# Row sums of a 64 MiB tensor: another split of the rows into a contiguous lead and a pitched body

## The chip, the cores and the metric

The kernel runs on one core of one Trainium2 chip. The metric is the device time of one execution in microseconds (us). Before the change three runs gave 160.83, 160.84 and 161.1 us, median 160.84.

The engines that matter here are VectorE (DVE in the profile), ScalarE (ACT), and SyncE (SP), which computes nothing and issues the transfers; sixteen DMA engines move the data between HBM and the on-chip memory of 128 partitions.

## What is computed

The reference sums the last axis of a float32 tensor and scales the sums:

```
batch, seq, dim = 32, 512, 1024
x = randn(batch, seq, dim).astype(float32);  multiplier = 0.5
out = (np.sum(x, axis=-1) * multiplier).astype(np.float32)
```

That is 16384 rows of 1024 numbers, 4 KiB a row, 67.1 MB to read and 64 KiB of results to write.

## The kernel before, in words

With 128 partitions each partition takes 128 rows. The rows are cut into two regions of the input. The first region has 112 rows per partition (`own`, line 42): partition p owns rows 112p to 112p+111, so that neighbouring partitions read at a pitch of 112 rows (448 KiB). The second region, `x_last`, is the contiguous end of the input, 16 rows per partition at a pitch of 16 rows (64 KiB).

The first region is read in seven blocks of B = 16 rows per partition (64 KiB a partition, 8 MiB a block). Three buffers `xb0` to `xb2` take turns. The loop of line 108 issues each block's load on SP (`load`, line 73, the DMA at line 76); from block 3 on a load first waits until VectorE has reduced the block that had the buffer before (`freed`). The first three loads wait for nothing, and `start_loads_at_entry` moves them into the entry of the program. All loads and stores are issued by SP and go through one queue in order of issue.

For each block VectorE waits for the load, reduces it in one instruction (line 121, 16 sums per partition into `sums`), and scales the sums into `res` (line 127). The seventh block is halved: VectorE reduces its first 8 rows, ScalarE the other 8, one row an instruction, as a scaled copy with an accumulator (`act_row`, line 85).

The last region is the tail, and is loaded in pieces, so that the work behind the last byte is small: 10 rows; 4 rows; one row and the first 384 columns of the last row (lines 146 to 158); then columns 384 to 735 of the last row, and columns 736 to 1023, both into the small tile `end` (lines 159 to 167). The waits at their issue keep buffer reuse in order: the tail's buffer must have been freed (line 143), the third piece's load waits for block 5's reduce, the last piece's for block 6's. In the tail VectorE and ScalarE share the rows. VectorE sums a row in one instruction that adds its two halves and accumulates (`dve_sum`, line 95); ScalarE has the rows in `on_act` (line 174). The last row is summed by VectorE in three cuts, the last of which also takes in the two partial sums, which lie in `end` just ahead of that cut's data (lines 185 to 192).

The results leave in two stores, both issued by SP. The early one (line 169) writes the 112 columns of the first region when block 6 has been summed. The last one (line 195) writes the 16 columns of the tail when the last sum is there. SP then waits for both to land (lines 199 and 200).

Of the kernel before, what the change touches and what calls it, by code (L numbers as in the profile page):

```python
# [8 lines left out]
@with_exitstack  # L9
def kernel(  # L10
    ctx: ExitStack,
    tc: tile.TileContext,
    x: bass.AP,
    multiplier: float,
    out: bass.AP,
):

    nc = tc.nc
    tc.close()
    tc.compile()  # L26
    nc.switch_body("work")

    P = nc.NUM_PARTITIONS
    fp32 = mybir.dt.float32  # L30
    ADD = mybir.AluOpType.add

    x_flat = x.flatten_outer_dims()
    N, D = x_flat.shape
    rows = N // P
    out_flat = out.rearrange("b s -> (b s)")
    mul = float(multiplier)

    B = 16
    n_blocks = rows // B  # L40
    assert N == P * rows and rows == n_blocks * B
    own = rows - B
    x_rows = x_flat[0 : P * own, :].rearrange("(p c) d -> p c d", p=P)
    x_last = x_flat[P * own : N, :].rearrange("(p c) d -> p c d", p=P)
    out_rows = out_flat[0 : P * own].rearrange("(p c) -> p c", p=P)
    out_last = out_flat[P * own : N].rearrange("(p c) -> p c", p=P)

    def sbuf(name, *shape):
        return ctx.enter_context(nc.sbuf_tensor(name, list(shape), fp32)).ap()

    bufs = 3
    buf = [sbuf(f"xb{i}", P, B, D) for i in range(bufs)]
    sums = sbuf("sums", P, rows)
    res = sbuf("res", P, rows)
    cuts = [384, 736, D]
    at = 368
    end = sbuf("end", P, at + D - cuts[1])

    def sem(name):
        return nc.alloc_semaphore(name=name)  # L60

    dve_done = sem("dve_done")
    act_done = sem("act_done")
    counts = {"dve": 0, "act": 0}

    def marks(i, engine):

        s = dve_done if engine == "dve" else act_done
        i.then_inc(s, 1)
        counts[engine] += 1  # L70
        return counts[engine]

    def load(name, dst, src, free=None, behind=None):

        landed = sem(name)
        i = nc.sync.dma_start(out=dst, in_=src)  # L76
        if free is not None:
            i.wait_op(dve_done, free, "sem-ge")
        if behind is not None:
            i.wait_op(behind, 16, "sem-ge")  # L80
        i.then_inc(landed, 16)
        return landed

    def act_row(t, r, col):
        return nc.scalar.activation(  # L85
            out=t[:, r, :],
            in_=t[:, r, :],
            func=mybir.ActivationFunctionType.Copy,
            scale=mul,
            accum_out=res[:, col : col + 1],  # L90
        )

    def dve_sum(row, dst, scale):
        mid = row.shape[-1] // 2
        return nc.vector.tensor_tensor_reduce(  # L95
            out=row[:, 0:mid],
            in0=row[:, 0:mid],
            in1=row[:, mid:],
            scale=scale,
            scalar=0.0,  # L100
            op0=ADD,
            op1=ADD,
            accum_out=dst,
        )

    freed = []
    blocks = []
    for b in range(n_blocks - 1):
        c0 = b * B
        t = buf[b % bufs]  # L110
        landed = load(
            f"landed{b}",
            t,
            x_rows[:, c0 : c0 + B, :],
            freed[b - bufs] if b >= bufs else None,
        )
        blocks.append(landed)
        h = B if b < n_blocks - 2 else B // 2
        nc.vector.wait_ge(landed, 16)
        done = marks(  # L120
            nc.vector.reduce_sum(  # L121
                out=sums[:, c0 : c0 + h], in_=t[:, 0:h, :], axis=mybir.AxisListType.X
            ),
            "dve",
        )
        freed.append(done)
        scaled = nc.vector.tensor_single_scalar(  # L127
            out=res[:, c0 : c0 + h],
            in_=sums[:, c0 : c0 + h],
            scalar=mul,  # L130
            op=mybir.AluOpType.mult,
        )
        scaled.wait_op(dve_done, done, "sem-ge")
        early_dve = marks(scaled, "dve")
        if h < B:
            nc.scalar.wait_ge(landed, 16)
            for r in range(h, B):
                i = act_row(t, r, c0 + r)
            early_act = marks(i, "act")

    c0 = (n_blocks - 1) * B
    t = buf[(n_blocks - 1) % bufs]
    nc.sync.wait_ge(dve_done, freed[n_blocks - 1 - bufs])
    flat = t.rearrange("p c d -> p (c d)")
    flat_last = x_last.rearrange("p c d -> p (c d)")
    bounds = [0, 10 * D, 14 * D, 15 * D + cuts[0]]

    landed = [
        load(f"landed_p{k}", flat[:, lo:hi], flat_last[:, lo:hi], free, behind)
        for k, (lo, hi, free, behind) in enumerate(  # L150
            zip(
                bounds[:-1],
                bounds[1:],
                (None, None, freed[n_blocks - 3]),
                (None, blocks[n_blocks - 3], None),
            )
        )
    ]
    landed_end = [
        load(f"landed_e{k}", end[:, to : to + hi - lo], x_last[:, B - 1, lo:hi], free, behind)  # L160
        for k, (to, lo, hi, free, behind) in enumerate(
            (
                (0, cuts[0], cuts[1], None, blocks[n_blocks - 2]),
                (at, cuts[1], D, freed[n_blocks - 2], None),
            )
        )
    ]
    nc.sync.wait_ge(dve_done, early_dve)
    early = nc.sync.dma_start(out=out_rows, in_=res[:, 0:own])
    early.wait_op(act_done, early_act, "sem-ge")  # L170
    early_stored = sem("early_stored")
    early.then_inc(early_stored, 16)

    on_act = {1, 4, 7, 9, 13, 14}
    for k, (lo, hi) in enumerate(((0, 10), (10, 14), (14, 15))):
        on = [r for r in range(lo, hi) if r in on_act]
        nc.scalar.wait_ge(landed[k], 16)
        for r in on:
            i = act_row(t, r, c0 + r)
        late_act = marks(i, "act") if k == len(landed) - 1 else None  # L180
        on = [r for r in range(lo, hi) if r not in on_act]
        nc.vector.wait_ge(landed[k], 16)
        for r in on:
            dve_sum(t[:, r, :], res[:, c0 + r : c0 + r + 1], mul)
    dve_sum(t[:, B - 1, 0 : cuts[0]], end[:, at - 2 : at - 1], 1.0)
    nc.vector.wait_ge(landed_end[0], 16)
    second = dve_sum(end[:, 0 : cuts[1] - cuts[0]], end[:, at - 1 : at], 1.0)

    second.then_inc(landed_end[1], 1)
    final = dve_sum(end[:, at - 2 :], res[:, rows - 1 : rows], mul)  # L190
    final.wait_op(landed_end[1], 17, "sem-ge")
    done = marks(final, "dve")

    nc.sync.wait_ge(act_done, late_act)
    store = nc.sync.dma_start(out=out_last, in_=res[:, own:])
    store.wait_op(dve_done, done, "sem-ge")
    stored = sem("stored")
    store.then_inc(stored, 16)
    nc.sync.wait_ge(early_stored, 16)
    nc.sync.wait_ge(stored, 16)  # L200

    def start_loads_at_entry(nc_):

        entry, *rest = nc_.main_func.blocks
        is_sp = lambda i: i.engine == mybir.EngineType.SP
        is_load = lambda i: type(i).__name__ == "InstDMACopy"
        for block in rest:
            body = list(block.instructions)  # L210
            own = [i for i in body if is_sp(i)]
            if not any(is_load(i) for i in own):
                continue
            lead = []
            for i in own:
                if not is_load(i) or i.sync_info.on_wait:
                    break
                lead.append(i)
            names = {i.name for i in lead}
            block.instructions = [i for i in body if i.name not in names]  # L220
            head = list(entry.instructions)
            at = next(
                k for k, i in enumerate(head) if is_sp(i) and type(i).__name__ == "InstDrain"
            )
            entry.instructions = head[:at] + lead + head[at:]
            return

    nc.at_finalize(start_loads_at_entry)
# [35 lines left out]
```

## Time and profile before

| | us |
|---|---|
| median of three runs | 160.84 |
| span of the profiled execution, first to last instruction | 159.3 |
| VectorE busy | 119.8 |
| ScalarE busy | 16.3 |
| VectorE waiting for blocks (line 121) | 33.3 in 7 waits |
| one block's reduce | 17.22 |
| scaling of a block's sums | 0.17 |
| a row on ScalarE, with its accumulator read | 1.04 |
| a row on VectorE in the tail, start to start | 0.61 |
| early store, issue to landing | 10.6 |
| last store, issue to landing | 1.4 |

The profile is of one execution; the time of that execution outside its span isn't given separately, and the median of the runs is 1.5 us above the span. In the rows, L121 is line 121 of the kernel, "xb<-in_x_dram" a transfer from the input into a buffer, and the bracket at the end of a timeline line tells how long the engine stood idle before the instruction and what it waited for. The digits are tenths of busy time in 40 slices of the span. Of SP, the profile shows the issues of transfers and what they waited for. TensorE isn't used.

### The profile page before, as it was taken

The page shows a single profiled execution, that of the slowest core. Times are in us where ns is not written, and L with a number is a line of the kernel's source. Part 1 is how long each engine was busy: PE and PEld are TensorE (multiplying, and loading weights), DVE is VectorE, ACT ScalarE, POOL GpSimd, SP SyncE. Part 2 cuts the span into 40 slices and gives each one's busy share as a digit, 9 for nine tenths or more (in the row PEclk, how much of TensorE's full clock was granted, in tenths as well). Part 3 has the DMA queues.
Part 4 walks back from the last instruction along what each step waited for, and adds up shares of the span by engine and source line. Part 5 has one row for each costly group of instructions (what it writes and reads, how often), then busy time and mean ns, then how long its engine had stood idle before and what let it go on. Part 6 is the DMA issues. An engine that isn't in the chain of part 4 may idle for free.

```text
span 159.3 us, 123 instructions
## 1 busy us (share of the span) xinstructions
DVE 119.8 (75%) x38; ACT 16.3 (10%) x29; POOL 0.2 (0%) x4
## 2 busy tenths in 40 slices
DVE  0000059998699968999599995999959999598376
ACT  3000000000000000000000000000000000397384
POOL 0000000000000000000000000000000000000000
DMA  7996996997998969969969969969989799798994
GB/s 263 526 526 263 526 526 263 526 477 313 526 428 362 526 280 510 526 263 526 526 263 526 526 263 526 494 296 526 444 345 526 345 444 526 329 473 350 424 396 151
DMA packets 2016, 67.18 MB, mean 422 GB/s; under 512 B 480, under 2 KB 736, under 8 KB 864
## 3 DMA queue, kind: packets, MB, share of 16 engines
q1 hardware_dynamic: 2016, 67.18, 98.1%
HBM read 67.11 MB, written 0.07 MB: 422 GB/s over the span
## 4 chain that ended last, share of the span: by engine, by line
DMA 74%; DVE 24%; another core or an unknown queue 1%; SPq 0%; issue 0%
DMA xb<-in_x_dram 74%; DVE sums L121 22%; DVE xb L95 1%; DVE end L95 0%; SPq L76 0%; DVE res L127 0%; DVE res L95 0%
## 5 line engine op out<-in xcount | busy, mean ns | idle before, releaser
L121 DVE TENSOR_REDUCE sums<-xb 128x16 f32<-128x16384 f32 (+1 forms) x7 | 112.0, 16001 | 33.3 <-DMA xb<-in_x_dram 33.3
L85 ACT ACTIVATE xb<-xb 128x1024 f32<-128x1024 f32 x14 | 14.6, 1044 | 139.1 <-DMA xb<-in_x_dram 139.1
L95 DVE CUSTOM_DVE_ANT_0 xb<-xb 128x512 f32<-128x512 f32 (+1 forms) x10 | 6.0, 655 | 4.4 <-DMA xb<-in_x_dram 4.4
L85 ACT ACTIVATION_READ_ACCUMULATOR xb<-xb 128x1 f32 x14 | 2.6, 187 | 0.0
L85 ACT ACT_TABLE_LOAD x1 | 1.3, 1283 | 2.4 <-PEq L26 2.4
L127 DVE TENSOR_SCALAR res<-sums 128x16 f32<-128x16 f32 (+1 forms) x7 | 1.2, 174 | 0.2
L95 DVE DVE_READ_ACCUMULATOR2_ANT res<- 128x1 f32 x10 | 0.8, 82 | 0.0
L95 DVE CUSTOM_DVE_ANT_0 end<-end 128x176 f32<-128x176 f32 (+1 forms) x2 | 0.7, 326 | 0.0
L95 DVE DVE_READ_ACCUMULATOR2_ANT end<- 128x1 f32 x2 | 0.2, 82 | 0.0
L245 POOL MEMSET const-bfloat16-1.0<- 128x1 bf16 x1 | 0.1, 101 | 0.0
L245 POOL MEMSET const-uint8-127<- 128x1 uint8 x1 | 0.1, 101 | 0.0
L245 POOL MEMSET const-float32-0.0<- 128x1 f32 x1 | 0.1, 98 | 0.2 <-issue 0.2
L245 POOL MEMSET const-float32-1.0<- 128x1 f32 x1 | 0.1, 98 | 0.0
## 6 DMA issues: line engine op xcount, KB each, us to landing
xb<-in_x_dram SPq DMA_DIRECT2D x1, 5120.0 KB, 33.6
xb<-in_x_dram SPq DMA_DIRECT2D x1, 2048.0 KB, 36.4
xb<-in_x_dram SPq DMA_DIRECT2D x1, 704.0 KB, 20.8
end<-in_x_dram SPq DMA_DIRECT2D x1, 176.0 KB, 19.2
end<-in_x_dram SPq DMA_DIRECT2D x1, 144.0 KB, 10.8
xb<-in_x_dram SPq DMA_DIRECT2D x7, 40.8
out_dram<-res SPq DMA_DIRECT2D x1, 56.0 KB, 10.6
out_dram<-res SPq DMA_DIRECT2D x1, 8.0 KB, 1.4
```

The lines of the kernel that those rows point to most:

```text
L85: return nc.scalar.activation(out=t[:, r, :], in_=t[:, r, :], func=mybir.ActivationFunctionType.Copy, scale=mul, accum_out=res[:, col : co ...
L95: return nc.vector.tensor_tensor_reduce(out=row[:, 0:mid], in0=row[:, 0:mid], in1=row[:, mid:], scale=scale, scalar=0.0, op0=ADD, op1=ADD, ...
L121: nc.vector.reduce_sum(out=sums[:, c0 : c0 + h], in_=t[:, 0:h, :], axis=mybir.AxisListType.X),
L127: scaled = nc.vector.tensor_single_scalar(out=res[:, c0 : c0 + h], in_=sums[:, c0 : c0 + h], scalar=mul, op=mybir.AluOpType.mult,)
L245: nc = _bacc.Bacc("TRN2", target_bir_lowering=False, num_devices=1)
```

## The change

The rows are split another way. The contiguous region now comes first and has 15 rows per partition (`lead`); it is block 0. The rest of the input is one region of 113 rows per partition (`body`) at a pitch of 113 rows (452 KiB). Its rows are read in six blocks of 16 rows and a tail of 17.

- The buffer that the tail is loaded into becomes a tile of 16 rows and 384 columns, `flat`; block buffers are still 16 rows.
- Block 0's load, reduce and scaling have 15 rows. Block 6 is halved into 8 and 8 rows as before.
- The tail's pieces are 11 rows, 4 rows, one row and 384 columns, and the two end pieces as before. ScalarE's rows are 1, 4, 7, 9, 14 and 15 of 17 instead of 1, 4, 7, 9, 13 and 14 of 16.
- The results leave in three stores: 96 columns of the body (384 B a partition at a pitch of 452 B), then the lead's 15 columns (60 B a partition, contiguous), and at the end the tail's 17 columns (68 B a partition at a pitch of 452 B). Before, each store's rows were contiguous in the output: 448 B and 64 B a partition. SP waits for one more landing at the end.

```diff
-    own = rows - B
-    x_rows = x_flat[0 : P * own, :].rearrange("(p c) d -> p c d", p=P)
-    x_last = x_flat[P * own : N, :].rearrange("(p c) d -> p c d", p=P)
-    out_rows = out_flat[0 : P * own].rearrange("(p c) -> p c", p=P)
-    out_last = out_flat[P * own : N].rearrange("(p c) -> p c", p=P)
+    lead = B - 1
+    tail = B + 1
+    body = rows - lead
+    x_lead = x_flat[0 : P * lead, :].rearrange("(p c) d -> p c d", p=P)
+    x_body = x_flat[P * lead : N, :].rearrange("(p c) d -> p c d", p=P)
+    out_lead = out_flat[0 : P * lead].rearrange("(p c) -> p c", p=P)
+    out_body = out_flat[P * lead : N].rearrange("(p c) -> p c", p=P)
...
-    buf = [sbuf(f"xb{i}", P, B, D) for i in range(bufs)]
+    cuts = [384, 736, D]
+    buf = [sbuf(f"xb{i}", P, B, D) for i in range(bufs - 1)]
+    flat = sbuf("xt", P, B * D + cuts[0])
+    buf.insert((n_blocks - 1) % bufs, flat[:, 0 : B * D].rearrange("p (c d) -> p c d", d=D))
...
-        c0 = b * B
         t = buf[b % bufs]
+        if b == 0:
+            c0, n, src = 0, lead, x_lead
+        else:
+            c0, n = lead + (b - 1) * B, B
+            src = x_body[:, c0 - lead : c0 - lead + B, :]
         landed = load(
             f"landed{b}",
-            t,
-            x_rows[:, c0 : c0 + B, :],
+            t[:, 0:n, :],
+            src,
             freed[b - bufs] if b >= bufs else None,
         )
...
-        h = B if b < n_blocks - 2 else B // 2
+        h = n if b < n_blocks - 2 else n // 2
...
-    c0 = (n_blocks - 1) * B
+    c0 = rows - tail
+    own = c0 - lead
...
-    flat = t.rearrange("p c d -> p (c d)")
-    flat_last = x_last.rearrange("p c d -> p (c d)")
-    bounds = [0, 10 * D, 14 * D, 15 * D + cuts[0]]
+    flat_last = x_body[:, own:body, :].rearrange("p c d -> p (c d)")
+    bounds = [0, 11 * D, 15 * D, B * D + cuts[0]]
...
-    early = nc.sync.dma_start(out=out_rows, in_=res[:, 0:own])
+    early = nc.sync.dma_start(out=out_body[:, 0:own], in_=res[:, lead:c0])
     early.wait_op(act_done, early_act, "sem-ge")
     early_stored = sem("early_stored")
     early.then_inc(early_stored, 16)
-
-    on_act = {1, 4, 7, 9, 13, 14}
-    for k, (lo, hi) in enumerate(((0, 10), (10, 14), (14, 15))):
+    first = nc.sync.dma_start(out=out_lead, in_=res[:, 0:lead])
+    first_stored = sem("first_stored")
+    first.then_inc(first_stored, 16)
+
+    on_act = {1, 4, 7, 9, 14, 15}
+    for k, (lo, hi) in enumerate(((0, 11), (11, 15), (15, 16))):
...
-    dve_sum(t[:, B - 1, 0 : cuts[0]], end[:, at - 2 : at - 1], 1.0)
+    dve_sum(flat[:, B * D :], end[:, at - 2 : at - 1], 1.0)
...
-    store = nc.sync.dma_start(out=out_last, in_=res[:, own:])
+    store = nc.sync.dma_start(out=out_body[:, own:], in_=res[:, c0:])
...
     nc.sync.wait_ge(early_stored, 16)
+    nc.sync.wait_ge(first_stored, 16)
     nc.sync.wait_ge(stored, 16)
```

## The prediction

> **What bounds the kernel now.** I read four views, in this order: the page's slices and queue rows (what is saturated), its chain of work (what the end hangs on), the timeline of VectorE (where the slack is), and SP's own waits (where the store issues sit).
>
> The page, slices of the span and the DMA queue:
>
> ```profile
> DVE  0000059998699968999599995999959999598376
> DMA  7996996997998969969969969969989799798994
> ...
> q1 hardware_dynamic: 2016, 67.18, 98.1%
> HBM read 67.11 MB, written 0.07 MB: 422 GB/s over the span
> ```
>
> The one queue keeps the sixteen DMA engines at work for 98.1% of the span, reading the input once. VectorE has a hole in every block. So transfers bound the kernel.
>
> The chain that ended last says the same, with its last steps:
>
> ```profile
> DMA 74%; DVE 24%; another core or an unknown queue 1%; SPq 0%; issue 0%
> ...
> 118.55 36.35 DMA xb<-in_x_dram
> 154.91 0.02 issue
> 154.93 0.69 DVE xb L95
> ...
> 157.12 0.36 DVE end L95 x3
> 157.48 0.02 issue
> 157.50 0.31 DVE end L95
> ```
>
> The 24% of VectorE are reduces that this chain runs through because they release a buffer for a later load; the freed loads wait in a queue that is not empty, so they don't set the pace. What does is visible in the timeline: a reduce starts when its block has landed.
>
> ```profile
> 21.81 17.22 DVE L121 TENSOR_REDUCE sums<-xb 128x16 f32<-128x16384 f32 x1 [21.81 <-DMA xb<-in_x_dram]
> 41.15 17.22 DVE L121 TENSOR_REDUCE sums<-xb 128x16 f32<-128x16384 f32 x1 [1.91 <-DMA xb<-in_x_dram]
> 60.50 17.22 DVE L121 TENSOR_REDUCE sums<-xb 128x16 f32<-128x16384 f32 x1 [1.92 <-DMA xb<-in_x_dram]
> ...
> 137.91 8.69 DVE L121 TENSOR_REDUCE sums<-xb 128x8 f32<-128x8192 f32 x1 [1.92 <-DMA xb<-in_x_dram]
> ...
> 150.03 0.69 DVE L95 CUSTOM_DVE_ANT_0 xb<-xb 128x512 f32<-128x512 f32 x1 [3.23 <-DMA xb<-in_x_dram]
> ...
> 154.93 0.69 DVE L95 CUSTOM_DVE_ANT_0 xb<-xb 128x512 f32<-128x512 f32 x1 [1.13 <-DMA xb<-in_x_dram]
> ```
>
> The starts are 19.35 us apart, with 1.9 us of idle each, so a block costs its transfer. 8.39 MB in 19.35 us are 433.5 GB/s. After block 6 (start 137.91) the 10-row piece takes 12.12 us to 150.03 and the 4-row piece 4.90 us to 154.93. From 16 and 4 rows: (19.35 - 4.90)/12 = 1.204 us a row, and 19.35 - 16 x 1.204 = 0.08 us for each load; 10 rows by that are 12.12, as measured. The pitch between partitions is 112 rows (448 KiB) for the blocks and 16 rows (64 KiB) for the last region, and one line fits both. The trace's records of single packets agree: nearly all 64 KiB packets of the seven blocks after the first round take 2.418 to 2.434 us, whatever their address.
>
> Last, SP's own waits:
>
> ```profile
> SPq L76 <- DVE res L127: 139.5, 7, 36.9
> SPq L194 <- ACT xb L85: 10.4, 1, 10.4
> SPq L200 <- DMA out_dram<-res: 1.1, 1, 1.1
> ```
>
> SP stands idle 10.4 us between the early store and the last one, and 1.1 us for the last store to land.
>
> **The change part by part.** The sum is made against the profiled execution: span 159.35 us (159.3 on the page). Its full time isn't given apart; the median of the runs, 160.84, lies 1.5 us above the span, which I keep.
>
> *The row moved from first block to tail.* Twelve loads before, twelve after, the same 67.11 MB. Block 0 has 15 rows: -1.204. The six others keep 19.35 each. The tail's first piece has 11 rows: +1.204. Second, third and the two end pieces are the same size. So block 0 lands at 20.6 rather than 21.8, every block up to block 6 lands 1.2 earlier (136.7), and the first tail piece lands at 150.0 as before. Sum 0.00; bounds from the fit, whose three rows agree within 0.01 us, ±0.05.
>
> The reuse waits keep their cover: block 3's load is issued when block 0's reduce ends (39.06), and the next place in the queue comes up when block 2 has arrived (60.5), 21 us later. All of it shifts by 1.2 us together; the reduce of block 0 gets 17.22/16 = 1.08 us shorter. If the cover were gone, a load would be late by a whole reduce. Likewise the last small load, which waits for block 6's half reduce, is issued at 145.4 rather than 146.6, with 11 us in the queue ahead of it.
>
> *One more row for VectorE in the first tail piece.* ScalarE keeps four rows there (1, 4, 7, 9), VectorE has seven instead of six. One is 0.61 us (150.03 to 150.65 to 151.26). It goes into the 1.13 us of idle before 154.93, leaving 0.52. Cost 0; were that cover gone, up to 0.61. Behind 154.93 the work is unchanged: three rows on VectorE, one on ScalarE, then 14 -> 15 on ScalarE and the three cut pieces.
>
> *The second early store.* SP issues it right after the first, 0.37 us by the row of the early store, in the 10.4 us hole: 0, and 0.37 if SP were needed there. On the DMA engines it adds 128 packets of 60 B behind the early store. Packets of 64 B took 0.008 to 0.011 us in the records, eight on an engine: 0.09 us. The order within the queue puts them behind all loads and the early store, whose packets end at 157.17 in the records; the last store's first packet starts at 158.73. So it lands by about 157.8 (the early one landed at 157.68) and has 1.5 us of room: 0, at most 0.1.
>
> *The wait for it.* One wait instruction on SP, 0.03 us by its neighbour's record; SP waits 1.1 us for the last store anyway, and nothing is queued behind it but that store's wait: 0.
>
> *The shape of the last store, which is on the path.* It wrote 64 B per partition into 8 KB on end; now 68 B at a pitch of 452 B, so starts no longer fall on multiples of 64 B. Before: issue 157.89, packets from 158.73 to 158.93, landed 159.30 (1.41 us). By size, packets of 64, 448 and 1152 B took 0.011, 0.025 and 0.051 us, so 4 B more are nothing. What shifted, scattered starts cost, the trace doesn't show. Upper end: each row is written as two packets and the landing needs one more trip like the extra of the first loads below, 0.09 + 0.69 = 0.78. Lower end: half of its 0.20 us of packets saved, -0.10. I take +0.02, since the aligned store with seven times the bytes, the nearest row, landed 0.51 us after its packets against 0.37: stores are insensitive here. The early store's shape changes too (384 B at 452 B), but it lands 1.6 us ahead of the end.
>
> Here a rule of the Trainium skill speaks against the change: in "DMA: Bandwidth & Descriptors", How a descriptor splits into AXI transactions, a descriptor that doesn't start on a 256 B boundary begins at the boundary below. Three in four of the old 64 B rows began off it already; of the new ones nearly all do, and some cross one. By the rule the sum would be higher by some nanoseconds a packet; no run so far shows a store at such starts.
>
> *The start.* The first 16-row block reaches VectorE at 21.81, 2.46 us more than the 19.35 of a later block. The packet records split that: 1.03 us from the first issue to the first packet, and a first round of packets that takes 2.42 to 3.42 us, on average 0.69 us longer than the others, with ends spread over 0.36 us. That spread stays to the end, since every engine then runs without a gap. The first addresses change: sixteen engines begin with partitions 60 KiB apart instead of 448 KiB. Lower end: the whole extra goes, -0.69. Upper end: the spread doubles, +0.36. I take 0: any first access has a way to go.
>
> **Sum**: 0 + 0 + 0 + 0 + 0.02 + 0 = +0.02 us; span 159.37, median 160.86.
>
> **The rivals.** (1) *The start gets shorter.* If the first round is slow because sixteen streams at the same 448 KiB pitch meet in the memory, a 60 KiB pitch spreads them, and what is saved stays saved: half is 160.84 - 0.35 = 160.5, all of it 160.15. For it: the first round alone is slow. Against: the later rounds at the same pitch are not slow, and the ends lie too close together for a long queue. The Trainium skill has the rule behind it ("DMA: Bandwidth & Descriptors", Latency and other measured facts: large power-of-two row pitches halve a copy's rate, 4 KiB of padding restore it); in the steady blocks the trace disagrees that anything is to be restored, at 433.5 GB/s with either pitch.
>
> (2) *Slower by the last store.* Place: the store of line 195, between its first packet (158.73) and the end. Writes of 68 B that straddle their neighbours' bytes need a read first; price 0.37 (one more landing) to 0.78, so 161.2 to 161.6. It decides from +0.3 us. For it: the path has no cover there, and rows of the early store share their lines with it. Against: seven times the bytes made little difference.
>
> (3) *The start gets worse*: +0.36, 161.2. (4) *The tail's VectorE is late*, or loads at 452 KiB or cut from a contiguous region run slower: 1% on the six blocks is +1.16, 162.0. Against: two pitches give one rate already.
>
> **How the numbers follow.** About 0.2%, 0.32 us, is what a measurement of this kernel can tell from no change (its three runs span 0.27). Forecast: 0.56, its own range 160.6 to 161.1. Shorter start 0.19. Last store 0.13, worse start 0.07, the others 0.05. So faster 0.19, same 0.56, slower 0.25. The range reaches halfway into both groups: 160.35 cuts off the fuller gains, about 0.1, and 161.35 the dearer half of the stores and the slow loads, about 0.1.
>
> **What would show it.** In the profile after: first reduce 128x15 of about 16.1 us, starting near 20.6; later starts 19.35 apart; the first tail sums at 150.0 and the idle before the second piece's sums down from 1.13 to 0.5; 2160 packets (2016 + 128 + the new store's 16 marks); the last store's landing 1.4 us. The prediction is wrong if the first reduce starts off 20.6 by over 0.3, if the pitch of starts isn't 19.35, or if the last landing takes over 1.7.

## The result and the profile after

The changed kernel takes 161.17 us (median of 16 runs, 161.01 to 161.31); the kernel before, 160.70 us, also in 16 runs (160.55 to 161.1). The ratio is 1.0025, with a 95% interval of 1.0019 to 1.0032. So it is slower by 0.47 us by the medians, beyond the 0.2% that the prediction took for no change, with the lower end of the interval just inside it.

The profiled execution took 161.21 us, with a span of 159.89 us against 159.35 before: 0.54 us more. First the page's slices and queue rows of the changed kernel, as they were shown of before:

```profile
DVE  0000079993899959999599995999959998695385
DMA  8999899899799799799799799899898997999893
...
q1 hardware_dynamic: 2160, 67.18, 97.8%
HBM read 67.11 MB, written 0.07 MB: 420 GB/s over the span
```

The packets are the 2160 that were expected, the bytes are the same, and the queue is still what is busy. Next the timeline of the changed kernel, the lines that answer to those of before (start, duration, what, and in brackets the idle time before it):

```profile
21.15 16.15 DVE L129 TENSOR_REDUCE sums<-xb 128x15 f32<-128x15360 f32 x1 [21.15 <-DMA xb<-in_x_dram]
40.48 17.22 DVE L129 TENSOR_REDUCE sums<-xt 128x16 f32<-128x16384 f32 x1 [2.96 <-DMA xt<-in_x_dram]
59.83 17.22 DVE L129 TENSOR_REDUCE sums<-xb 128x16 f32<-128x16384 f32 x1 [1.92 <-DMA xb<-in_x_dram]
...
137.24 8.69 DVE L129 TENSOR_REDUCE sums<-xb 128x8 f32<-128x8192 f32 x1 [1.93 <-DMA xb<-in_x_dram]
...
150.56 0.69 DVE L99 CUSTOM_DVE_ANT_0 xt<-xt 128x512 f32<-128x512 f32 x1 [4.43 <-DMA xt<-in_x_dram]
...
155.45 0.69 DVE L99 CUSTOM_DVE_ANT_0 xt<-xt 128x512 f32<-128x512 f32 x1 [0.52 <-DMA xt<-in_x_dram]
...
158.00 0.31 DVE L99 CUSTOM_DVE_ANT_0 end<-end 128x145 f32<-128x145 f32 x1
158.42 0.33 SPq L206 DMA_DIRECT2D out_dram<-res  x1
```

The first reduce was forecast for 20.6 and starts at 21.15, 0.55 us late. From there the later starts are 19.33 to 19.36 us apart, as before. The 11 rows of the first tail piece take 13.32 us (137.24 to 150.56), which is what 12.12 + 1.20 makes. VectorE's idle time before the second piece is 0.52 us, as forecast. The last sum starts at 158.00 instead of 157.50. So the whole loss is there when the first block lands, and is carried nearly unchanged to the end (0.54 us in the span).

The chain of the changed kernel ends in

```profile
135.12 22.05 DMA xt<-in_x_dram
157.18 0.02 issue
157.20 1.15 ACT xt L89 x2
```

with ScalarE's last row rather than VectorE's last sum. They end within 0.03 us of each other (158.35 and 158.32), as they nearly did before, so this is no new bound. SP's waits show that the added store is hidden as forecast:

```profile
SPq L205 <- ACT xt L89: 11.1, 1, 11.1
SPq L212 <- DMA out_dram<-res: 1.0, 1, 1.0
```

Why is the first block late? The trace's records of single packets show it. The block is 128 packets; by their times each of the sixteen DMA engines moves eight of them, without a gap between them. The first packets of the sixteen engines end between 4.16 and 4.53 us before, 0.36 us apart; in the changed kernel between 3.70 and 4.94 us, 1.25 us apart. On average they are hardly late: 4.27, where 4.32 less 0.15, the difference between a packet of 60 KiB and one of 64 KiB, would be 4.17. But the slowest engine is now 0.67 us behind the mean instead of 0.21. The trace holds sixteen landing marks for every load, and a load has landed with the last of them, so the slowest engine decides. The two terms, 0.10 for the mean and 0.46 for the slowest, make 0.56; the first reduce is 0.55 late. As all engines have the same work from then on, the spread is still there at the end: the sixteen landing marks of block 6 span 0.35 us before and 1.11 us after. Between 157 and 158 us only stragglers and small stores are at work; the windows of before and of after (columns: length, then busy time of VectorE, ScalarE and GpSimd with instructions, clock, DMA share, GB/s):

```profile
157.00:158.00 1.00, 0.79 (x6) 0.82 (x2) 0.00 (x0) 1.00 0.04 9
```

```profile
157.00:158.00 1.00, 0.97 (x6) 0.80 (x1) 0.00 (x0) 1.00 0.22 56
```

The DMA share of this microsecond rises from 0.04 to 0.22.

### The profile page after: what moved, and what is told of

Same layout as the page of the kernel before. It is cut to its first block, busy times and chain, and to the rows that moved or that the text cites. A ratio compares the mean times of both kernels' runs of the same rounds, so it can differ in the third digit from the quotient of the medians.

```text
span 159.9 us, 127 instructions
## 1 busy us (share of the span) xinstructions
DVE 119.4 (75%) x40; ACT 16.3 (10%) x29; POOL 0.2 (0%) x4
## 2 busy tenths in 40 slices
DMA packets 2160, 67.18 MB, mean 420 GB/s; under 512 B 624, under 2 KB 880, under 8 KB 1008
## 3 DMA queue, kind: packets, MB, share of 16 engines
q1 hardware_dynamic: 2160, 67.18, 97.8%
## 4 chain that ended last, share of the span: by engine, by line
DMA 64%; DVE 32%; another core or an unknown queue 1%; ACT 1%; SPq 0%; issue 0%
DMA xt<-in_x_dram 39%; DVE sums L129 32%; DMA xb<-in_x_dram 26%; ACT xt L89 1%; SPq L80 0%; DVE res L135 0%
## 5 line engine op out<-in xcount | busy, mean ns | idle before, releaser
L129 DVE TENSOR_REDUCE sums<-xb 128x16 f32<-128x16384 f32 (+2 forms) x5 | 76.5, 15299 | 28.9 <-DMA xb<-in_x_dram 28.9
L129 DVE TENSOR_REDUCE sums<-xt 128x16 f32<-128x16384 f32 x2 | 34.4, 17220 | 4.9 <-DMA xt<-in_x_dram 4.9
L89 ACT ACTIVATE xb<-xb 128x1024 f32<-128x1024 f32 x8 | 8.3, 1042 | 133.6 <-DMA xb<-in_x_dram 133.6
L99 DVE CUSTOM_DVE_ANT_0 xt<-xt 128x512 f32<-128x512 f32 (+1 forms) x11 | 6.6, 657 | 4.9 <-DMA xt<-in_x_dram 4.9
L89 ACT ACTIVATE xt<-xt 128x1024 f32<-128x1024 f32 x6 | 6.3, 1048 | 6.1 <-DMA xt<-in_x_dram 6.1
L89 ACT ACTIVATION_READ_ACCUMULATOR xb<-xb 128x1 f32 x8 | 1.5, 187 | 0.0
L135 DVE TENSOR_SCALAR res<-sums 128x16 f32<-128x16 f32 (+2 forms) x7 | 1.2, 174 | 0.2
L89 ACT ACTIVATION_READ_ACCUMULATOR xt<-xt 128x1 f32 x6 | 1.1, 186 | 0.0
```

The lines of the kernel that those rows point to most:

```text
L89: return nc.scalar.activation(out=t[:, r, :], in_=t[:, r, :], func=mybir.ActivationFunctionType.Copy, scale=mul, accum_out=res[:, col : co ...
L99: return nc.vector.tensor_tensor_reduce(out=row[:, 0:mid], in0=row[:, 0:mid], in1=row[:, mid:], scale=scale, scalar=0.0, op0=ADD, op1=ADD, ...
L129: nc.vector.reduce_sum(out=sums[:, c0 : c0 + h], in_=t[:, 0:h, :], axis=mybir.AxisListType.X),
L135: scaled = nc.vector.tensor_single_scalar(out=res[:, c0 : c0 + h], in_=sums[:, c0 : c0 + h], scalar=mul, op=mybir.AluOpType.mult,)
```

## The experiments

The change does two things to the first load at once, its pitch and its size, and it changes the stores. The theory at the outset was that the pitch makes the start uneven; the rivals were the size of the load and the stores. Four kernels first, each beside runs of the kernel before on the same chip.

**Only the pitch of the first load undone.** Block 0's 15 rows come from the body:

```diff
-            c0, n, src = 0, lead, x_lead
+            c0, n, src = 0, lead, x_body[:, 0:lead, :]
```

> The changed kernel with one edit: block 0's 15 rows per partition are read from the body, at a pitch of 452 KiB, instead of from the contiguous lead at 60 KiB (so 1920 of the sums are those of other rows; sizes, instructions and stores are those of the changed kernel). Theory 'pitch of the first load': the sixteen engines end their first round within about 0.4 us instead of 1.25 us, the first reduce starts near 20.6 instead of 21.15, and the time is near that of before: ratio to before 0.999 to 1.001. Rival 'size of the first load' (60 KiB packets): first reduce stays at 21.15, ratio 1.0025. Rival 'stores': first reduce stays wherever it is, last store over 1.5 us, ratio 1.0025.

The first reduce:

```profile
20.63 16.15 DVE L129 TENSOR_REDUCE sums<-xb 128x15 f32<-128x15360 f32 x1 [20.63 <-DMA xb<-in_x_dram]
```

It starts at 20.63, where the prediction had put it, with the first round's ends 0.52 us apart. Size alone is not the cause. Yet the time is 160.93 us, ratio 1.0013 (1.0004 to 1.0022), and not fully that of before. In the profile the rest is lost at the very end of this kernel:

```profile
157.15 0.34 DVE L99 CUSTOM_DVE_ANT_0 end<-end 128x176 f32<-128x176 f32 x1
157.81 0.31 DVE L99 CUSTOM_DVE_ANT_0 end<-end 128x145 f32<-128x145 f32 x1 [0.31 <-DVE end L99]
```

The last sum starts 0.66 us after the one before it, against 0.38 before and after the change. The last small load landed 0.66 us after the one ahead of it (157.79 and 157.13; the early stores of 384 and 60 B stand behind it in the queue), although its data packets had ended at 157.06, little later than the 156.99 of before.

**The first load contiguous in the kernel before.**

```diff
-            x_rows[:, c0 : c0 + B, :],
+            x_rows[:, c0 : c0 + B, :] if b else x_last,
```

> The kernel before with one edit: block 0's 16 rows per partition are read from the contiguous region, at a pitch of 64 KiB instead of 448 KiB (so its 2048 sums are those of other rows). Theory 'pitch of the first load': a low pitch spreads the engines' ends, the first reduce starts at 22.2 to 22.5 instead of 21.8, ratio to before 1.002 to 1.004. Rivals 'size of the first load' and 'stores': nothing changes, 21.8 and ratio 1.000.

Measured: first reduce at 21.97, ends 0.56 us apart, 160.82 us, ratio 1.0007 (0.9998 to 1.0016). A miss: a low pitch does little harm by itself. 64 KiB and 60 KiB are not alike.

**The changed kernel with its first two blocks in the other order.** This one computes everything.

```diff
-        if b == 0:
+        if b == 1:
             c0, n, src = 0, lead, x_lead
         else:
-            c0, n = lead + (b - 1) * B, B
+            c0, n = lead + max(b - 1, 0) * B, B
```

> The changed kernel with its first two blocks in the other order: 16 rows of the body first (452 KiB), the contiguous 15 rows second; everything is still computed, and all three stores are those of the changed kernel. Theory 'pitch of the first load': the first reduce starts near 21.8, the second near 39.9 to 40.0, ratio to before 0.999 to 1.001. Rival 'size of the first load': also back to before, since the 60 KiB packets are no longer first. Rival 'contiguous block costs wherever it stands': second reduce at 40.5, ratio 1.0025. Rival 'stores': ratio 1.0025 with the reduces on time.

```profile
21.92 17.22 DVE L129 TENSOR_REDUCE sums<-xb 128x16 f32<-128x16384 f32 x1 [21.92 <-DMA xb<-in_x_dram]
40.05 16.15 DVE L129 TENSOR_REDUCE sums<-xt 128x15 f32<-128x15360 f32 x1 [0.70 <-DMA xt<-in_x_dram]
```

160.90 us, ratio 1.0010 (1.0001 to 1.0019). The contiguous block costs 18.13 us in second place, 15 rows by 1.204 and 0.08: nothing lost. So the 60 KiB load harms only as the first. By the medians over half of the changed kernel's loss is gone.

**The row's move alone.** The regions stay as before, with 111 rows at 444 KiB and a contiguous tail of 17; the stores have contiguous rows:

```diff
-    x_lead = x_flat[0 : P * lead, :].rearrange("(p c) d -> p c d", p=P)
-    x_body = x_flat[P * lead : N, :].rearrange("(p c) d -> p c d", p=P)
+    own = rows - tail
+    x_rows = x_flat[0 : P * own, :].rearrange("(p c) d -> p c d", p=P)
+    x_last = x_flat[P * own : N, :].rearrange("(p c) d -> p c d", p=P)
...
-            c0, n, src = 0, lead, x_lead
+            c0, n, src = 0, lead, x_rows[:, 0:lead, :]
```

> The row's move alone: regions as before, but 111 rows per partition at a pitch of 444 KiB and a contiguous tail of 17; block 0 has 15 rows of the first region, two stores with contiguous rows as before (444 B and 68 B a partition). Theory 'pitch of the first load': first reduce near 20.6, ratio to before 0.999 to 1.001. Rival 'size of the first load': first reduce at 21.15 and ratio 1.0025. Rival 'stores of the new shapes': ratio 1.000 with a last store of 1.41 us.

```profile
21.01 16.15 DVE L129 TENSOR_REDUCE sums<-xb 128x15 f32<-128x15360 f32 x1 [21.01 <-DMA xb<-in_x_dram]
```

The first reduce is at 21.01, with the ends 0.92 us apart, and the time is 161.21 us, ratio 1.0031 (1.0020 to 1.0043). The theory in its first form has fallen: neither a contiguous source nor a new store is in this kernel, and it is as slow as the changed one. By these kernels it could still be size (with an exception at 452 KiB), or the pitch in another way. I took the first addresses of neighbouring engines to lie four partitions apart within each half of eight engines, which the Trainium skill states ("DMA: Bandwidth & Descriptors", The descriptor swizzle) and no run here shows; the prediction had put them one partition apart. Over that distance, 60 and 444 KiB make a step of -16 KiB from a multiple of 64 KiB, 452 one of +16, and 64 and 448 none. The next two set size against step.

**16 rows at 444 KiB in the kernel before:**

```diff
+    x_444 = x_flat[0 : P * (own - 1), :].rearrange("(p c) d -> p c d", p=P)
...
-            x_rows[:, c0 : c0 + B, :],
+            x_rows[:, c0 : c0 + B, :] if b else x_444[:, 0:B, :],
```

> The kernel before with one edit: block 0's 16 rows are read at a pitch of 444 KiB instead of 448 KiB (its sums are those of other rows). Theory 'address step': the start is slow where the engines' first addresses, four partitions apart, step by 48 KiB modulo 64 KiB (60 and 444 KiB), and not where they step by 0 or 16 KiB (64, 448, 452 KiB). It expects a first reduce at 22.2 to 22.4 instead of 21.8 and ratio 1.002 to 1.004. Rival 'size': only 60 KiB packets start badly (with an exception at 452 KiB): 21.8 to 21.9, ratio 1.000. Rival 'chance of the build': any value from 21.8 to 22.4, in no order.

```profile
22.41 17.22 DVE L122 TENSOR_REDUCE sums<-xb 128x16 f32<-128x16384 f32 x1 [22.41 <-DMA xb<-in_x_dram]
41.73 17.22 DVE L122 TENSOR_REDUCE sums<-xb 128x16 f32<-128x16384 f32 x1 [1.89 <-DMA xb<-in_x_dram]
```

One row less in the pitch of one load, and the first reduce starts 0.60 us later; the time is 161.23 us, ratio 1.0027 (1.0016 to 1.0037). That is the whole size of the change's loss, with the packets of before, 64 KiB.

**15 rows at 448 KiB instead of 444 in the kernel with the row's move alone:**

```diff
-            c0, n, src = 0, lead, x_rows[:, 0:lead, :]
+            c0, n, src = 0, lead, x_448[:, 0:lead, :]
```

> The kernel with 15 rows in block 0 and a contiguous tail of 17, with block 0 read at 448 KiB instead of 444 KiB (a row too few is summed at each partition's edge, and others twice). Theory 'address step': first reduce back to 20.6 to 20.7, ratio 1.000. Rival 'size': 21.0 to 21.15 and ratio 1.0025 to 1.003, as at 444 KiB.

```profile
20.76 16.15 DVE L130 TENSOR_REDUCE sums<-xb 128x15 f32<-128x15360 f32 x1 [20.76 <-DMA xb<-in_x_dram]
```

160.77 us, ratio 1.0003 (0.9994 to 1.0011): the loss is gone, with 60 KiB packets in place. The start is a little later than the 20.6 to 20.7 expected. Size is out as the cause of these starts; between 444 and 448 KiB the pitch of the first load does it, in both directions.

**The stores.** Two kernels part the stores from the loads: the changed kernel with block 0 at 452 KiB and the old stores, and the kernel before with the new stores alone.

```diff
-    early = nc.sync.dma_start(out=out_body[:, 0:own], in_=res[:, lead:c0])
+    early = nc.sync.dma_start(out=out_rows, in_=res[:, 0:c0])
...
-    first = nc.sync.dma_start(out=out_lead, in_=res[:, 0:lead])
...
-    store = nc.sync.dma_start(out=out_body[:, own:], in_=res[:, c0:])
+    store = nc.sync.dma_start(out=out_last, in_=res[:, c0:])
```

> The changed kernel with block 0 read at 452 KiB and the stores as before in shape: one early store of 111 contiguous columns, a last one of 17 (part of the sums are of other rows or at other places). Theory 'pitched early stores': in the run at 452 KiB with the new stores the last small load landed 0.66 us after the one before it instead of 0.37, because the early stores of 384 and 60 B come in while the slower engines still mark that load; without them it lands 0.37 to 0.40 later, ratio to before 1.000. Rival 'pitch of the last load': 1152 B at 452 KiB mark late by themselves, 0.66 stays and ratio 1.0013.

160.79 us, ratio 1.0006 (0.9997 to 1.0015); the last sum starts 0.38 us after the one before it.

```diff
-    early = nc.sync.dma_start(out=out_rows, in_=res[:, 0:own])
+    early = nc.sync.dma_start(out=out_body[:, 0 : own - B], in_=res[:, lead : own - 1])
...
+    first = nc.sync.dma_start(out=out_lead, in_=res[:, 0:lead])
...
-    store = nc.sync.dma_start(out=out_last, in_=res[:, own:])
+    store = nc.sync.dma_start(out=out_body[:, own - B :], in_=res[:, own - 1 :])
```

> The kernel before with the changed kernel's three stores and nothing else of it (96 columns at a pitch of 452 B, 15 columns, at the end 17 columns at 452 B; some sums go to other places). Theory 'pitched early stores': the last small load lands 0.5 to 0.7 us after the one before it, ratio to before 1.001 to 1.002, last store 1.41 us from issue to landing. Rival 'pitch of the last load': 0.37, ratio 1.000.

```profile
157.15 0.34 DVE L97 CUSTOM_DVE_ANT_0 end<-end 128x176 f32<-128x176 f32 x1
157.54 0.31 DVE L97 CUSTOM_DVE_ANT_0 end<-end 128x145 f32<-128x145 f32 x1
157.92 0.33 SPq L200 DMA_DIRECT2D out_dram<-res  x1
```

160.71 us, ratio 0.9998 (0.9989 to 1.0007). The theory that the pitched early stores delay the last load's landing marks fell in its plain form: beside loads of the old pitch they cost nothing. The stores by themselves are out with it as a cause; the last store takes 1.42 us.

One more kernel takes the lead's store out of the first experiment, by deleting its three lines and the wait for it:

> The changed kernel with block 0 read at 452 KiB as in the first of these runs, and without the lead's store (those 15 columns are not written out). The last small load landed 0.66 us after the one before it with both early stores, 0.35 with one contiguous store. Theory 'the 384 B store at 452 B is enough': 0.55 to 0.7 here, ratio 1.001 to 1.002. Rival 'the 60 B store behind it, or a chance of that run': 0.35 to 0.40, ratio 1.0000 to 1.0006.

The last sum starts 0.38 us after the one before it (157.31 and 157.69), 160.82 us, ratio 1.0008 (0.9999 to 1.0017). So 0.66 was seen once, and 0.46 once, in the kernel with swapped blocks; both have the tail at 452 KiB and both early stores. So has the changed kernel, whose profile shows 0.38. The three kernels that lack one of these show 0.38. The times, 1.0013 and 1.0010 against 1.0006 and 1.0008, overlap in their intervals. What holds the marks back there stays open, and so does a chance of those two executions. It is no part of the 0.54 us in the changed kernel's profile.

**How far the rule of the step goes.** The kernel before, with block 0's 16 rows at 440 and at 456 KiB (the edit as at 444):

> The kernel before, block 0's 16 rows read at 440 KiB (its sums are those of other rows): first addresses of neighbouring engines step by 32 KiB modulo 64 KiB, by -32 KiB modulo 256 KiB. Theory 'steps below zero': every pitch a few rows under a multiple of 64 KiB starts badly; first reduce 22.2 to 22.4 and ratio 1.002 to 1.004. Rival 'only the step of 48 modulo 64': 21.8 to 22.0 and ratio 1.000 to 1.001.

```profile
22.29 17.22 DVE L122 TENSOR_REDUCE sums<-xb 128x16 f32<-128x16384 f32 x1 [22.29 <-DMA xb<-in_x_dram]
```

> The kernel before, block 0's 16 rows read at 456 KiB (its sums are those of other rows): steps of 32 KiB modulo 64 KiB, of +32 modulo 256 KiB. Theory 'steps below zero': no harm, first reduce 21.8 to 22.0, ratio 1.000 to 1.001. Rival 'steps other than 0 or 16 modulo 64 KiB': 22.2 to 22.4, ratio 1.002 to 1.004, the same as at 440 KiB.

```profile
22.04 17.22 DVE L122 TENSOR_REDUCE sums<-xb 128x16 f32<-128x16384 f32 x1 [22.04 <-DMA xb<-in_x_dram]
```

440 KiB: 161.12 us, ratio 1.0027 (1.0017 to 1.0038), as the theory had it. 456 KiB: 161.03 us, ratio 1.0019 (1.0010 to 1.0028), a miss, since it expected at most 1.001; the rival expected the same as at 440 and has the lateness in the profile, 0.23 us against 0.48, against it. The sign of the step matters less than the theory had it: 8 KiB above a multiple of 64 KiB there is a loss too.

All first loads together. "Late" is the first reduce against 21.81 for 16 rows and 20.61 for 15; "ends" is how far apart the engines' first packets end, from the packet records. Both are of one profiled execution of each kernel; the ratio is of the medians of its runs:

| pitch, KiB | from a multiple of 64 | rows | late, us | ends, us | ratio |
|---|---|---|---|---|---|
| 448 (before) | 0 | 16 | 0 | 0.36 | 1 |
| 448 (before, new stores) | 0 | 16 | 0.04 | 0.43 | 0.9998 |
| 448 | 0 | 15 | 0.15 | 0.59 | 1.0003 |
| 64 | 0 | 16 | 0.16 | 0.56 | 1.0007 |
| 452, four kernels | +4 | 15, 16 | 0.02 to 0.17 | 0.45 to 0.61 | 1.0006 to 1.0013 |
| 456 | +8 | 16 | 0.23 | 0.73 | 1.0019 |
| 440 | -8 | 16 | 0.48 | 0.93 | 1.0027 |
| 444 | -4 | 15, 16 | 0.40, 0.60 | 0.92, 1.13 | 1.0031, 1.0027 |
| 60 (after) | -4 | 15 | 0.54 | 1.25 | 1.0025 |

A chance of the single build isn't ruled out by a second build of any of these kernels, but kernels with the same pitch fall together (three at 448 KiB, four at 452, two at 444), which speaks against it.

**What the first round's extra belongs to.** The kernel before with block 0's load in two, one row and then fifteen:

```diff
+        s = 0 if b else 1
+        if s:
+            nc.vector.wait_ge(load("landed_s", t[:, 0:s, :], x_rows[:, 0:s, :]), 16)
...
-            t,
-            x_rows[:, c0 : c0 + B, :],
+            t[:, s:B, :],
+            x_rows[:, c0 + s : c0 + B, :],
```

> The kernel before with block 0's load in two, one row per partition and then fifteen; everything is computed. It asks what the first round's extra of 0.69 us belongs to. Theory 'first access': each engine's first packet pays it whatever its size; the first reduce starts 0.08 later for the added load, 21.9, ratio 1.0005. Rival 'the streams meet': with first packets of 4 KiB the engines part before the long packets start, and up to 0.3 us are saved: 21.5 to 21.7, ratio 0.998 to 0.9995.

First reduce at 21.85, 160.73 us, ratio 1.0006 (0.9997 to 1.0015). First packets of 4 KiB save nothing that can be measured. The start is where the theory had it, but the packet records don't show that each engine's first packet pays. Per engine the eight packets of 4 KiB take 1.80 us, 0.53 more than eight of the later 0.159; in the kernel before one 64 KiB packet has 0.68 too much (the 0.69 of the prediction). By the times at which one packet ends and the next starts, four engines have a short first packet (0.22 to 0.32 us) and then a second of 0.35 to 0.83. And in the kernel before, the engine that starts last, at 1.96 us, takes 2.42 us, with no extra at all. So the extra lies at the start of the stream and isn't saved by short packets; what it belongs to stays open. None of the twelve kernels is measurably faster than the kernel before.

## Why the prediction was wrong in its likeliest case

It forecast 160.86 us and no change with 0.56, and gave slower 0.25. The time, 161.17, lies in its range, and slower by over 0.2% is what came. By its own sign the prediction was wrong: the first reduce starts 0.55 us off 20.6, and 0.3 was allowed. That the time is in the range is partly luck, since the range reached up to 161.35 for dearer stores and slow loads, which didn't come. So is the 161.2 of its third rival: it stands on 160.84, the median of three runs, and 160.70 in sixteen would have made it 161.06.

- *The start* is the step that failed. "I take 0: any first access has a way to go", with an upper end of +0.36 for a doubled spread. It measured +0.54 in the profiled execution, with a spread of 0.36 grown to 1.25, more than threefold. Its split of the 2.46 us names 1.03 and 0.69 and leaves about 0.75: by the same records the engines start 0.19 later than the first of them on average, the slowest ends 0.21 behind the mean, and 0.35 lie between the last packet and the landing. The 0.21 is the term that the change raised, to 0.67. The direction and the mechanism, a worse start whose spread stays to the end, were the third rival, at 0.07, with its price too low. That the pitch of the first load alone does this was shown both ways: 448 to 444 KiB costs 0.60 us at the first reduce, 444 to 448 gives it back. For the changed kernel's own 60 KiB the run at 452 KiB gave back 0.52 of 0.54 there; in the time only about half came back (ratio 1.0013 against 1.0025), and the rest, late landing marks at the end in its profile, isn't explained.
- The first rival, a shorter start, had the same place and the wrong sign. Its reasoning, that streams at 448 KiB meet in the memory, is not borne out: the two pitches that are multiples of 64 KiB are among the best starts. The rule of the Trainium skill named beside it ("DMA: Bandwidth & Descriptors", Latency and other measured facts: 4 KiB of padding restore a pitch that is a large power of two) finds no support in these starts, where 4 KiB less was among the worst and 4 KiB more no gain; but it is stated for copies between HBM tensors at 512 KiB and above, which no run here has, and 448 KiB is no power of two.
- *The row moved*: right. The bounds of ±0.05 hold from the first reduce on; every later step is on its forecast plus the 0.5.
- *VectorE's added row*: right, the idle time is 0.52.
- *The second early store and the wait for it*: right for this kernel. Its issue took 0.44 us in a hole of 11.1, and it landed at 158.38, before the last store's first packet at 159.25. Tried alone the three stores gave 0.9998.
- *The last store*: right, +0.02. From issue to landing it took 1.43 us (158.42 to 159.85) against 1.41, and its packets of 68 B took 0.009 to 0.012 us each, where those of 64 B took 0.008 to 0.011. The second rival, at 0.13, fell.

The error behind the number was to look at the first round's mean, 0.69 us, and to treat the spread as an accident. In a kernel that a stream of transfers bounds without a gap, the slowest engine's start is part of the time.

## What to carry to other kernels

Where transfers bound a kernel from the first packet to the last, look at how far apart the DMA engines' first packets end: here the spread of 1.14 us between the first block's landing marks was still 1.11 at block 6. The row pitch of the first load was worth up to 0.3% here, and the contiguous block in second place cost nothing extra; so put a load first whose pitch has been tried and starts the engines evenly, and change the order of the blocks before changing the layout. A 0.5 us shift at the first landing that all later stages carry unchanged points at the start, whatever else the change touches.

## What the runs showed that was not expected

- Of the loads tried here only the first is sensitive. In steady state packets of 64 KiB take 2.42 us at 448 KiB and at 452 KiB pitch, and the contiguous 60 KiB block costs its bytes when it is second (18.13 us). Why the start depends on the pitch, with the worst cases of those tried 4 to 8 KiB below a multiple of 64 KiB, was not found; the step between engines' first addresses orders the table only roughly, and the four partitions between neighbouring engines were taken over, not shown.
- The engines' lateness isn't spread evenly. At 60 KiB the first packets end earlier than before on the best engine (3.70 against 4.16 us) and later on the worst (4.94 against 4.53), though a packet is 0.15 us shorter there.
- A load can land late though its data came on time: 157.06 for the last packet and 157.79 for the landing, where 0.48 us lay between before. Fourteen of its sixteen marks came by 157.44, the last two at 157.67 and 157.79. It was seen in two kernels and left open.
